# A two-layer conformer/attention trunk in fp32: other gate units of the second layer form their low parts by an adding transfer, with more raw tiles and one more weight pair

## Chip, cores and metric

One Trainium2 chip, one NeuronCore. The kernel is a single launch. The metric is the device time of that launch in microseconds (us); lower is better. Engines are named as in the profile: PE is TensorE (matmul), PEld its weight loads, DVE is VectorE, ACT is ScalarE, POOL is GpSimd, SP is SyncE, which here only issues transfers.

## What is computed

Two layers over 256 latent tokens and 256 context tokens, width 1024, all in float32. Each layer mixes tokens and then channels:

```python
h = modulate(rmsnorm(x, norm1_g[l]), sh1, sc1)
p = h @ w_in[l]                      # GLU | q, k, v | 2 x 1024 gate columns
q, k = rope_2d(q, ...), rope_2d(k, ...)
y_conv = conv_branch(p[..., :GLU_END], ...)      # GLU, depthwise conv of 31 taps, LayerNorm, swish, projection
y_attn = merge_heads(neighbourhood_attention(q, k, v, k_c, v_c, na_rpb[l])) @ w_na_out[l]
x = x + g1 * gated_merge(p[..., QKV_END:], y_conv, y_attn, w_out[l])
...
def gated_merge(p_gate, y_conv, y_attn, w_o):
    g_conv, g_attn = jnp.split(jax.nn.sigmoid(p_gate), 2, axis=-1)
    return (g_conv * y_conv + g_attn * y_attn) @ w_o
...
h2 = modulate(rmsnorm(x, norm2_g[l]), sh2, sc2)
x = x + g2 * conv_ffn(h2, w_up[l], ffn_dw[l], ffn_dw_b[l], w_down[l])
```

Context tokens go through the same weights in the first layer; in the second (the last) only their keys and values are needed. A final RMSNorm follows.

## The kernel before, in words

**Weights as units.** All weights of a layer are cut into 118 units of 128 x 1024 float32 (512 KB each), in the order in which they are used: two units of the first GLU group, four of V, thirty of the input projection (`U_IN + t`: t 0 to 5 the other GLU groups, 6 to 9 Q, 10 to 13 K, 14 to 29 the sixteen gate units), then the attention's and the conv branch's output projections (4 each), the output projection (8), up (44) and down (22).

**A product in three matmuls.** A float32 product is formed from operands split in a high part (rounded to fp32r) and a low part (the rest). `mm3` (lines 196 to 199) issues three matmuls for each 128 x 128 block: high by high (L197), high by low (L198), low by high (L199). The activations `h` are kept split; a weight unit is split when it has been loaded.

**The two ways to split a weight.** `wparts` (lines 157 to 177): SP loads the unit into a raw tile, ScalarE casts it into `whi` (L167), VectorE subtracts, `wlo = raw - whi` (L168). `wadded` (lines 211 to 219): ScalarE casts (L216), ScalarE negates the high part into `wlo` (L217), and POOL issues a transfer that adds the raw tile to `wlo` (L218); VectorE has no part in it. `unit8` picks the second way for the units in the set `ADDED` (line 47). In layer 1 these are t = 7, 8 (Q, units 1 and 2) and 16 (gate 2).

**Tiles.** The pool `w` has four raw tiles, four `whi` and four `wlo`, which all units use in turn: a new unit takes a slot when its last reader has gone. The first four up units of the second layer get their pairs from that stage's own pool `ef1` instead (argument `at`), so that all four stand at once. Each stage opens a pool of its own over the same space: `ea1` (mixing stage of layer 1: conv sums `cb`, attention outputs `oh`, `ol`, the rope table, conv inputs `u`, gates), inside it `eb1` and `ec1`, then `ef1` (feed-forward); `ef0` is the feed-forward of layer 0.

**The order of the work.** A framework orders each engine's instructions ahead of time: it takes the program's order as the priority and lets a later instruction pass an earlier one that is not ready in its own reckoning. It also sets the semaphores. On the chip each engine runs its list in order.

**Around the change.** Layer 1 begins with the two units of the first GLU group (`sc` banks), the other GLU groups, V, then Q and K of four head pairs. Between them and after them come the sixteen gate units, which fill TensorE while the attention steps wait for softmax. The 31 x 4 conv taps run on VectorE (L673) all through this stage, a few at each `slot()`. Then the attention's projection (the gates are multiplied in at L993), the layer norm of the conv branch (its first sums on POOL, L949 and L950; the sum of squares over partitions at L370), the conv projection and the merges (L998 to L1001), the output projection with residuals (L1007) and squares (L352, L356), and the feed-forward, whose first four units run on `h2` before its norm is known (L1109) and get the norm's factor later.

Of the kernel before, what the change touches and what calls it, by code (L numbers as in the profile page):

```python
# [8 lines left out]
F32 = mybir.dt.float32  # L9
F32R = mybir.dt.float32r  # L10
# [5 lines left out]
P = 128  # L16
# [15 lines left out]
UW = 1024  # L32
# [11 lines left out]

U_GLU0, U_V, U_IN, U_NA, U_CO, U_WO, U_UP, U_DN = 0, 2, 6, 36, 40, 44, 52, 96
NU = 118
ADDED = {*((0, U_IN + i) for i in (*range(19), 20, 22, 24, 26, 28)), *((0, u) for u in (U_NA + 1, U_NA + 3, *range(U_CO, U_CO + 4))), *((1, U_IN + i) for i in (7, 8, 16))}
T_GLU, T_Q, T_K, T_GATE = 0, 6, 10, 14

SWAP16 = [(i + 16) % 32 for i in range(32)]  # L50
# [3 lines left out]
def trunk(ctx: ExitStack, tc: tile.TileContext, xt, cvec, crow, wall, wada, params, bias_t, rope_t, out):  # L54
# [6 lines left out]
    wp = ctx.enter_context(tc.tile_pool(name="w", bufs=1))  # L61
# [6 lines left out]
    def nm(s):  # L68
        uid[0] += 1
        return f"{s}_{uid[0]}"  # L70
# [6 lines left out]
    def tmp(w=512):  # L77
        return tp.tile([P, w], F32, tag="t", bufs=5, name=nm("t"))
# [70 lines left out]

    lastdma = [None]  # L150

    def raw_unit(src, r=None):
        r = wp.tile([P, UW], F32, tag="raw", bufs=4, name=nm("raw")) if r is None else r
        lastdma[0] = sp.dma_start(r, src)
        return r

    def wparts(l, u, at=None, cuts=2):

        r = wp.tile([P, UW], F32, tag="raw", bufs=4, name=nm("raw"))
        hi = (at or wp).tile([P, UW], F32R, tag="whi", bufs=4, name=nm("whi"))  # L160
        lo = (at or wp).tile([P, UW], F32R, tag="wlo", bufs=4, name=nm("wlo"))
        cs = [slice(i * UW // cuts, (i + 1) * UW // cuts) for i in range(cuts)]
        for c in cs:
            lastdma[0] = sp.dma_start(r[:, c], wall[l, u][:, c])

        def split(c):
            act.copy(hi[:, c], r[:, c])  # L167
            dve.tensor_tensor(lo[:, c], r[:, c], hi[:, c].bitcast(F32), ALU.subtract)  # L168

        def more():  # L170
            for c in cs[1:]:
                split(c)

        split(cs[0])
        return (hi, lo), more

    def wunit(l, u, at=None, cuts=1):
        w, more = wparts(l, u, at, cuts)
        more()
        return w  # L180

    def cols(w, i):
        return sl(w[0], i), sl(w[1], i)
# [27 lines left out]
    def wadded(l, u):  # L211

        r = raw_unit(wall[l, u])
        hi = wp.tile([P, UW], F32R, tag="whi", bufs=4, name=nm("whi"))
        lo = wp.tile([P, UW], F32R, tag="wlo", bufs=4, name=nm("wlo"))
        act.copy(hi, r)  # L216
        act.mul(lo, hi.bitcast(F32), -1.0)  # L217
        pool.dma_start(lo, r, accum_op=ALU.add)  # L218
        return hi, lo

    def unit8(l, u, at=None):
        w = wadded(l, u) if (l, u) in ADDED else wunit(l, u, at)
        return [cols(w, i) for i in range(KD)]
# [12 lines left out]
    def ada_products(l, j, bank, place=lambda: None, after=None):  # L236

        ps = psum(bank)
        for u in range(2):
            r = raw_unit(wada[l, 2 * j + u], place())  # L240
            with tc.issue_after(after.ins) if after else ExitStack():
                ada_half(ps, u, r)
        return ps
# [45 lines left out]
    def ada_dots(l, tiles, sb, place=lambda: None, early=0):  # L289


        left, tiles, units = 0, list(tiles), []
        for i, n in enumerate(tiles):
            for m in tiles[len(units) : i + early]:
                units.append(raw_unit(wada[l, m], place()))
            while left < len(sb):
                yield
                left += pace[0]
            left -= len(sb)
            if not early:  # L300
                units.append(raw_unit(wada[l, n], place()))
            r = units[i]
            for s, v in enumerate(sb):
                dve.tensor_tensor_reduce(  # L304
                    tmp().bitcast(BF16), r, v, 1.0, pr(l, BADA + n, 1), ALU.mult, ALU.add, mods[l][:, n, s : s + 1]
                )
# [325 lines left out]
    for l in range(DEPTH):  # L632
        last = l == DEPTH - 1
# [3 lines left out]

        with ExitStack() if last else start as e1a:
            ea = e1a.enter_context(tc.tile_pool(name=f"ea{l}", bufs=1)) if last else ea0
            cb = [ea.tile([P, NS, S], F32, name=f"cb{l}_{j}") for j in range(KC)]  # L640
            oh = [ea.tile([P, T], F32R, name=f"oh{l}_{j}") for j in range(4)]
            ol = [ea.tile([P, T], F32R, name=f"ol{l}_{j}") for j in range(4)]
# [282 lines left out]
            with ExitStack() as e1c:  # L925
# [57 lines left out]
                def branch(base, xh, xl):  # L983
                    for n in range(0, KD, 2):
                        w = (wadded if (l, base + n // 2) in ADDED else wunit)(l, base + n // 2)
                        for i in range(2):
# [9 lines left out]
                for n, pc in branch(U_CO, sh_, sl_):  # L996
                    t = tmp()[:, :T]
# [56 lines left out]
                        add_side(nl)  # L1054


        with ExitStack() as e2:
            ef = e2.enter_context(tc.tile_pool(name=f"ef{l}", bufs=1))
            if not last:
# [43 lines left out]
            if last:  # L1103
# [14 lines left out]
                for i, ps in enumerate(pss):  # L1118
                    b = small([P, 1], "wb", 4)
                    act.copy(b, ps[:, S : S + 1])  # L1120
                    u = ef.tile([P, S], F32, name=f"u{l}_{i}")
# [48 lines left out]
            for streams, ns in [((0, 1), range(NB)), *(((s,), range(NB, KD)) for s in range(NS))]:  # L1170
                wu = None
                c = slice(streams[0] * S, (streams[-1] + 1) * S)
                for n in ns:
                    ps = psum()
                    for k in range(KF):
                        t = n * KF + k
# [166 lines left out]
```

## Time and profile before

| | us |
|---|---|
| median of 3 runs | 1063.33 (1061.96 to 1065.06) |
| the profiled execution | 1063.1 |
| its span, first to last instruction | 1061.3 |
| granted TensorE clock | 0.996 |

How the profile is read: "busy" is the time in which an engine had an instruction under way. Matmuls are pipelined, so a busy TensorE may still be slower than it could be; the number of matmuls in a stretch tells its rate. In rows of groups, `main<-h,whi` says which tile is written from which, with the buffer numbers left out; `xN` is the count. In rows of the timeline the first two numbers are start and duration in us, and `[0.55 <-DVE qk L882]` is the idle time ahead of the instruction and what ended it. In rows of windows the numbers in brackets are counts, and after the engines come the granted clock, the share of the transfer engines and GB/s. Rows of waits give total, number and longest.

### The profile page before, as it was taken

The numbers are of one execution on the slowest core, as the hardware profiler recorded it, in microseconds if no ns is written. First come the engines' busy times: TensorE is split into PE (matmuls) and PEld (weight loads), VectorE is DVE, ScalarE is ACT, GpSimd is POOL, SyncE is SP. The second block draws the span as 40 slices with busy tenths as digits, with TensorE's granted clock in tenths as the row PEclk, the third lists the DMA queues.
The fourth block names the chain that finished last, engine by engine and source line by source line (L and its number), as shares of the span: only waits on it lengthen the run. The fifth ranks groups of instructions, "written<-read, shape, count | busy, mean of one in ns | idle before, by whom it ended". The sixth has DMA issues, their size and how long they took to land.

```text
span 1061.3 us, 18038 instructions
## 1 busy us (share of the span) xinstructions
PE 1033.7 (97%) x6886; PEld 932.5 (88%) x6886; DVE 893.3 (84%) x1630; ACT 567.4 (53%) x943; POOL 43.6 (4%) x59
## 2 busy tenths in 40 slices
PE   8999999999999999999989999999999999999997
PEld 6787788888879988888878889999889999999997
DVE  5568898988998798898888547899899988988883
ACT  4458767545334544443433223545776666767652
POOL 1111110011000000000000000000000000000000
PEclk9999999999999999999999999999999999999998
DMA  9988665889943344564556657666734484666781
GB/s 373 304 227 229 150 153 138 260 247 245 290 149 118 101 159 160 165 190 142 186 186 218 210 189 233 208 210 196 216 117 144 159 283 155 199 205 193 230 286 61
DMA packets 59510, 209.26 MB, mean 197 GB/s; under 512 B 7200, under 2 KB 7456, under 8 KB 59424
## 3 DMA queue, kind: packets, MB, share of 16 engines
q1 hardware_dynamic: 54384, 190.77, 54.5%
q0 software_dynamic: 4752, 17.30, 8.5%
q8 instruction: 54, 0.88, 0.3%
q14 instruction: 32, 0.26, 0.1%
q10 hardware_dynamic: 288, 0.04, 0.0%
HBM read 187.63 MB, written 1.05 MB: 178 GB/s over the span
## 4 chain that ended last, share of the span: by engine, by line
PE 39%; issue 34%; DVE 16%; ACT 5%; DMA 4%; SPq 1%; POOL 0%; DVEq 0%; ACTq 0%; POOLq 0%
PE main L197 10%; PE main L198 10%; PE main L199 10%; PE main L736 4%; DVE cb L673 4%; DMA raw<-in_wall 3%; DVE wlo L168 3%; DVE t L304 2%; SPq L728 1%; ACT whi L167 1%; PE po L230 1%; DMA own<-in_wada 1%; DVE t L403 1%; DVE h L1001 1%; DVE t L999 1%
## 5 line engine op out<-in xcount | busy, mean ns | idle before, releaser
L199 PE MATMUL main<-h,wlo 128*128 128x256 f32 (+1 forms) x1328 | 430.7, 325 | 6.6 <-DVE wlo L168 6.6
L197 PE MATMUL main<-h,whi 128*128 128x256 f32 (+1 forms) x1328 | 433.5, 327 | 1.8 <-DVE qk L882 1.2
L198 PE MATMUL main<-h,whi 128*128 128x256 f32 (+1 forms) x1328 | 430.9, 325 | 1.6 <-DVE h L1001 1.4
L167 ACT CAST whi<-raw 128x1024 fp32r<-128x1024 f32 (+1 forms) x211 | 217.6, 1036 | 230.9 <-DMA raw<-in_wall 143.9
L168 DVE TENSOR_TENSOR wlo<-raw,whi 128x1024 fp32r<-128x1024 f32 (+1 forms) x211 | 252.5, 1205 | 71.7 <-ACT whi L167 70.7
L199 PEld LDWEIGHTS main<-h,wlo 128*128 128x128 f32 x1328 | 252.8, 191 | 24.9 <-DVE wlo L168 8.0
L197 PEld LDWEIGHTS main<-h,whi 128*128 128x128 f32 x1328 | 253.2, 191 | 22.9 <-issue 1.5
L198 PEld LDWEIGHTS main<-h,whi 128*128 128x128 f32 x1328 | 253.0, 191 | 19.6 <-DVE h L1001 2.1
L673 DVE SCALAR_TENSOR_TENSOR cb<-u,par,cb 128x512 f32<-128x512 f32 (+1 forms) x240 | 144.4, 617 | 2.8
L199 PE MATMUL main<-fh,wlo 128*128 128x256 f32 (+1 forms) x386 | 119.4, 309 | 0.0
L198 PE MATMUL main<-fl,whi 128*128 128x256 f32 (+1 forms) x386 | 119.3, 309 | 0.0
L197 PE MATMUL main<-fh,whi 128*128 128x256 f32 (+1 forms) x386 | 119.3, 309 | 0.0
L304 DVE CUSTOM_DVE_ANT_0 t<-raw,sb,par 128x1024 bf16<-128x1024 f32 x72 | 91.5, 1278 | 0.5 <-ACT sb L284 0.3
L199 PEld LDWEIGHTS main<-fh,wlo 128*128 128x128 f32 x386 | 73.7, 191 | 3.8 <-DVE wlo L168 0.4
L198 PEld LDWEIGHTS main<-fl,whi 128*128 128x128 f32 x386 | 73.7, 191 | 3.4
L197 PEld LDWEIGHTS main<-fh,whi 128*128 128x128 f32 x386 | 73.7, 191 | 3.4
L304 DVE CUSTOM_DVE_ANT_0 t<-own,sb,par 128x1024 bf16<-128x1024 f32 x48 | 60.4, 1279 | 2.2 <-DMA own<-in_wada 2.2
L216 ACT CAST whi<-raw 128x1024 fp32r<-128x1024 f32 x33 | 34.6, 1047 | 40.3 <-PE main L198 34.2
L1070 ACT ACTIVATE t<-main,par 128x512 f32<-128x512 f32 (+1 forms) x82 | 50.6, 666 | 5.4 <-PE main L199 5.4
L1071 DVE SCALAR_TENSOR_TENSOR t<-main,par,t 128x510 f32<-128x510 f32 (+1 forms) x82 | 47.4, 613 | 1.3 <-ACT t L1070 1.0
L1074 DVE SCALAR_TENSOR_TENSOR t<-main,par,t 128x510 f32<-128x510 f32 (+1 forms) x82 | 46.7, 611 | 0.0
L404 ACT ACTIVATE h<-t,mod 128x256 fp32r<-128x256 f32 x56 | 25.2, 501 | 33.8 <-DVE t L403 33.6
(216 smaller groups left out, 1254.7 us busy)
## 6 DMA issues: line engine op xcount, KB each, us to landing
raw<-in_wall SPq DMA_DIRECT2D x240, 512.0 KB, 4.4
raw<-in_wada SPq DMA_DIRECT2D x64, 512.0 KB, 4.4
wlo<-raw POOLq DMA_DIRECT2D x33, 512.0 KB, 5.6
own<-in_wada SPq DMA_DIRECT2D x24, 512.0 KB, 6.2
bias<-in_bias_t SPq DMA_DIRECT2D x8, 520.0 KB, 5.1
row<-in_wada SPq DMA_DIRECT2D x8, 512.0 KB, 4.8
sb<-in_crow SPq DMA_DIRECT2D x5, 512.0 KB, 4.8
x<-in_xt SPq DMA_DIRECT2D x4, 512.0 KB, 5.1
```

The costliest lines, as they stand in the source:

```text
L167: act.copy(hi[:, c], r[:, c])
L168: dve.tensor_tensor(lo[:, c], r[:, c], hi[:, c].bitcast(F32), ALU.subtract)
L197: pe.matmul(ps, w[0], order(xh), start=start, stop=False)
L198: pe.matmul(ps, w[0], order(xl), start=False, stop=False)
L199: pe.matmul(ps, w[1], order(xh), start=False, stop=stop)
L216: act.copy(hi, r)
L304: dve.tensor_tensor_reduce(tmp().bitcast(BF16), r, v, 1.0, pr(l, BADA + n, 1), ALU.mult, ALU.add, mods[l][:, n, s : s + 1])
L673: dve.scalar_tensor_tensor(cb[j], src, w, cb[j], ALU.mult, ALU.add)
L736: mm = pe.matmul(pv[t], h1[n == 1][k][:, c], runs(w[n == 2][:, b]), start=k + n == 0, stop=k == KD - 1 and n == 2)
L1070: act.activation(c, pv_, AF.Identity, bias=pr(l, FDB + t, 1), scale=w[1])
L1071: dve.scalar_tensor_tensor(c[:, :, 1:], pv_[:, :, : S - 1], w[0], c[:, :, 1:], ALU.mult, ALU.add)
L1074: dve.scalar_tensor_tensor(c[:, :, : S - 1], pv_[:, :, 1:], w[2], c[:, :, : S - 1], ALU.mult, ALU.add)
```

## The change

It does three things in layer 1.

- `ADDED` gets t = 15, 17, 19, 21, 23, 25, 27, 29 (the gate units with an odd n) and loses t = 16 (gate 2).
- A function `raw_tile` hands out raw tiles. While the mixing stage of layer 1 is being written, calls whose running number is 1, 3 or 5 modulo 7 get one of three more raw tiles in `ea1`; the others get one of the four in `w`.
- A function `split_tiles` hands out pairs. In the same stretch, every fifth call gets a pair in `ea1` (one buffer), the others one of the four in `w`.

The running numbers count all calls from the start of the program.

```diff
-ADDED = {..., *((1, U_IN + i) for i in (7, 8, 16))}
+ADDED = {..., *((1, U_IN + i) for i in (7, 8, *range(15, 30, 2)))}
...
+    more_w = [None]
+    count = [0, 0]
+
+    def raw_tile():
+        count[0] += 1
+        more = more_w[0] is not None and count[0] % 7 in (1, 3, 5)
+        return (more_w[0] if more else wp).tile([P, UW], F32, tag="raw", bufs=3 if more else 4, name=nm("raw"))
+
+    def split_tiles(at=None):
+        count[1] += 1
+        more = at is None and more_w[0] is not None and count[1] % 5 == 0
+        return [
+            (at or (more_w[0] if more else wp)).tile([P, UW], F32R, tag=t, bufs=1 if more else 4, name=nm(t)) for t in ("whi", "wlo")
+        ]
+
     def raw_unit(src, r=None):
-        r = wp.tile([P, UW], F32, tag="raw", bufs=4, name=nm("raw")) if r is None else r
+        r = raw_tile() if r is None else r
...
     def wparts(l, u, at=None, cuts=2):
-        r = wp.tile([P, UW], F32, tag="raw", bufs=4, name=nm("raw"))
-        hi = (at or wp).tile([P, UW], F32R, tag="whi", bufs=4, name=nm("whi"))
-        lo = (at or wp).tile([P, UW], F32R, tag="wlo", bufs=4, name=nm("wlo"))
+        r = raw_tile()
+        hi, lo = split_tiles(at)
...
     def wadded(l, u):
         r = raw_unit(wall[l, u])
-        hi = wp.tile([P, UW], F32R, tag="whi", bufs=4, name=nm("whi"))
-        lo = wp.tile([P, UW], F32R, tag="wlo", bufs=4, name=nm("wlo"))
+        hi, lo = split_tiles()
...
             ea = e1a.enter_context(tc.tile_pool(name=f"ea{l}", bufs=1)) if last else ea0
+            more_w[0] = ea if last else None
...
+        more_w[0] = None
         with ExitStack() as e2:
```

More of the change, by code (lines that the diff above doesn't have):

```diff
@@ L46 @@
 NU = 118
-ADDED = {*((0, U_IN + i) for i in (*range(19), 20, 22, 24, 26, 28)), *((0, u) for u in (U_NA + 1, U_NA + 3, *range(U_CO, U_CO + 4))), *((1, U_IN + i) for i in (7, 8, 16))}
+ADDED = {*((0, U_IN + i) for i in (*range(19), 20, 22, 24, 26, 28)), *((0, u) for u in (U_NA + 1, U_NA + 3, *range(U_CO, U_CO + 4))), *((1, U_IN + i) for i in (7, 8, *range(15, 30, 2)))}
 T_GLU, T_Q, T_K, T_GATE = 0, 6, 10, 14
```

## The prediction, on record before the result

> **What bounds the kernel now.** I read the page first, then the rate of TensorE, then each stage of layer 1 by windows, then what TensorE itself waited for, and last the single places.
>
> ```profile
> span 1061.3 us, 18038 instructions
> PE 1033.7 (97%) x6886; PEld 932.5 (88%) x6886; DVE 893.3 (84%) x1630; ACT 567.4 (53%) x943; POOL 43.6 (4%) x59
> q0 software_dynamic: 4752, 17.30, 8.5%
> wlo<-raw POOLq DMA_DIRECT2D x33, 512.0 KB, 5.6
> 950.00:1000.00 50.00, 50.00 (x450) 50.00 (x449) 42.78 (x74) 34.18 (x55) 0.00 (x0) 1.00 0.66 202
> 703.50:740.10 36.60, 36.60 (x219) 33.38 (x218) 36.56 (x80) 15.73 (x23) 0.92 (x1) 1.00 0.57 173
> 740.10:823.00 82.90, 81.51 (x748) 74.42 (x747) 77.76 (x186) 59.15 (x126) 4.04 (x4) 1.00 0.52 160
> 869.60:889.30 19.70, 18.23 (x152) 17.33 (x150) 16.50 (x34) 11.15 (x26) 0.70 (x1) 1.00 0.60 204
> ```
>
> The profiled execution took 1063.1 us around its span of 1061.3; the median of the runs shown, 1063.33, is 0.2 higher. In the last stretch of the feed-forward, 450 matmuls of 256 columns fill 50 us at full clock: 0.111 us each, TensorE's peak here. A gate unit of layer 1 has 24 of them, 2.67 us. From 740 to 823, where the sixteen gates and the attention lie, VectorE is busy for 77.76 of 82.90 us (94%), ScalarE for 59.15 (71%), the transfer engines for 52%. VectorE looks like the bound of this stage. But TensorE has 81.51 of the 82.90, and from 703.5 to 740.1 VectorE is full (36.56 of 36.60) without costing it anything. So the next question is what TensorE waited for.
>
> ```profile
> PE pt L370 <- DVE ss L356: 1.8, 2, 1.0
> PE main L199 <- DVE wlo L168: 1.3, 2, 0.9
> PE main L197 <- DVE qk L882: 1.2, 2, 0.6
> 769.38 0.46 PE L197 MATMUL main<-h,whi 128*128 128x512 f32 x1 [0.55 <-DVE qk L882]
> 784.88 0.38 PE L197 MATMUL main<-h,whi 128*128 128x256 f32 x1 [0.64 <-DVE qk L882]
> 829.79 0.60 PE L370 MATMUL pt<-one,ss 128*128 128x1 f32 x4 [0.97 <-DVE ss L356]
> 848.51 0.38 PE L199 MATMUL main<-h,wlo 128*128 128x256 f32 x1 [0.89 <-DVE wlo L168]
> 871.40 0.38 PE L199 MATMUL main<-h,wlo 128*128 128x258 f32 x1 [0.42 <-DVE wlo L168]
> 877.99 0.61 PE L370 MATMUL pt<-one,ss 128*128 128x1 f32 x4 [0.85 <-DVE ss L356]
> ```
>
> The first three rows are the waits of TensorE from 740 to 900, the others their places. All of it is VectorE, and all of it is 4.3 us. A late VectorE costs little because TensorE runs behind a stock of prepared weights. That is the ceiling of what the edit can win in its own stage; about 0.3% of the time, 3.2 us, is what a measurement of this kernel can tell from no change.
>
> **The change part by part: the gate units.** Eight gate units (n odd) lose their subtraction on VectorE, and gate 2, which had been without it, gets it back: seven net. The rows are the durations of a cast, the negation, the issue and the subtraction.
>
> ```profile
> L216 ACT CAST whi<-raw x33: 1027/1045/1087, 43.1 to 748.2; 128x1024 fp32r<-128x1024 f32 x33
> L217 ACT ACTIVATE wlo<-whi x33: 1042/1057/1099, 44.2 to 749.3; 128x1024 fp32r<-128x1024 f32 x33
> L218 POOL DMA_DIRECT2D wlo<-raw x33: 852/862/1058, 45.6 to 750.8; - x33
> L168 DVE TENSOR_TENSOR wlo<-raw,whi x69: 1207/1219/1231, 659.1 to 895.2; 128x1024 fp32r<-128x1024 f32 x69
> DMA to landing us min/median/max: 4.4/5.6/10.9
> ```
>
> VectorE gives up 7 x 1.22 = 8.5 us, ScalarE takes 7 x 1.06 = 7.4 us (59.15 becomes 66.6 of 82.9, 80%), POOL 7 x 0.86 = 6 us of issuing. The 33 transfers of before hold 8.5% of the span, 2.7 us of all sixteen engines each; seven more are 19 us, and the share of 0.52 becomes about 0.75. No engine becomes full.
>
> What of the 8.5 us reaches TensorE? Only the four places from 769 to 849. The one at 769.38 lies behind gate 1 (1.22 less) and gate 2 (1.22 more): no relief, 0.55 stays. The one at 784.88 follows gate 3, those at 829.79 and 848.51 follow all eight. I take 0.64 + 0.97 + 0.89 = 2.5 us as the gain. Bounds: 3.05 if 769.38 goes too; 0 if the two later ones are chains of their own (squares to root, then the burst of merges).
>
> **Is a transferred low part in time?** Cast, negation, issue and landing are 1.05 + 1.06 + 0.86 + 5.6 = 8.6 us, against 1.05 + 1.22 for a subtracted one. With four pairs a cast can start when TensorE leaves the unit four back, 3 x 2.67 = 8.0 us ahead of need; with five it is 10.7. The one example in this stage, unit 1 of Q, with four pairs:
>
> ```profile
> 732.27 1.03 ACT L216 CAST whi<-raw 128x1024 fp32r<-128x1024 f32 x1
> 734.80 0.92 POOL L218 DMA_DIRECT2D wlo<-raw  x1 [41.07 <-DVE cb L673]
> 740.52 0.38 PE L199 MATMUL main<-h,wlo 128*128 128x256 f32 x1
> SPq L164 <- DMA wlo<-raw: 9.3, 2, 5.5
> ```
>
> It was ready at about 740.5, 8.2 us after its cast began, just when TensorE came. Five pairs leave 2 us over, so I cost the longer way at nothing; the cover is those four units, and without it each transferred unit would cost 0.6 us, at the longest landing (10.9) 3.2 us. The last row is SP: raw loads queue behind a raw tile that an adding transfer still reads. With seven raw tiles instead of four, that wait has three more loads in front of it; I cost it at nothing too. On POOL the two sums of the layer norm (L949, L950) wait for the taps and stand in the same queue; whatever is issued behind them waits too.
>
> The Trainium skill (DMA: Bandwidth & Descriptors, section "Anatomy of one DMA — SWDGE (gpsimd) path") gives such a transfer 2.0 us plus its bytes at 436 GB/s, 3.2 us for 512 KB; the trace has 5.6, and by 3.2 the fifth pair would not be needed and the sum would stay as it is. A rule against the change is in SBUF — State Buffer, section "SBUF: two separate sides": VectorE in a two-port mode keeps GpSimd from writing descriptors, which would lead to rival 3. The trace shows no sign of it: VectorE at 94%, yet no issue longer than 1.06 us.
>
> **The new tiles and their pool.** The three raw tiles and the pair come from ea1, the pool of layer 1's mixing stage, whose space earlier belonged to ef0 (feed-forward of layer 0) and later to ef1. How a pool changes hands is in the trace:
>
> ```profile
> 686.71 0.28 PE L199 MATMUL main<-fhl,wlo 128*128 128x256 f32 x1
> 687.01 0.33 SPq L827 DMA_DIRECT2D rope<-in_rope_t  x1
> 849.23 0.42 DVE L999 TENSOR_TENSOR t<-t,g 128x256 f32<-128x256 f32 x1
> 849.73 0.33 SPq L282 DMA_DIRECT2D sb<-in_crow  x1
> SPq L282 <- DVE t L999: 0.8, 1, 0.8
> ```
>
> The rope table, the first load into ea1, leaves 0.02 us after the end of the last matmul that reads ef0; `sb`, the first load into ef1, leaves when the last gate of layer 1's mixing stage has been read, and waited for exactly that. I read it as a hold on the whole pool. Then two places pay.
>
> **Start of layer 1.** Pairs are counted from the first call: layer 0 makes 123 (118 units, less two that are taken by hand, plus 7 down units read twice), so layer 1 has 124 to 175, and raw tile 175 is its first. The second unit of the first GLU group is raw 176 and pair 125: both in ea1, not to be touched before 686.99.
>
> ```profile
> raw<-in_wall SPq DMA_DIRECT2D x240, 512.0 KB, 4.4
> 687.60 1.05 ACT L167 CAST whi<-raw 128x1024 fp32r<-128x1024 f32 x1 [2.31 <-DMA raw<-in_wall]
> 688.68 1.23 DVE L168 TENSOR_TENSOR wlo<-raw,whi 128x1024 fp32r<-128x1024 f32 x1
> 689.50 0.28 PE L197 MATMUL sc<-h,whi 128*128 128x256 f32 x1
> ```
>
> Its load leaves behind rope's at about 687.4, lands at 691.8, is cast by 692.9 and subtracted by 694.1; before, the pair was ready at 689.9 and TensorE came at 689.50. If TensorE's order stayed, it would stand 694.1 - 689.5 - 0.2 (two matmuls with the high part) = 4.4 us. But the next unit (raw 177, pair 126, both in the old pool) takes the freed place at 687.60, is ready at 689.9, and its 2.67 us fit in between, up to 692.6; the one after fits partly. The order of instructions is made by a scheduler that takes what is ready, as layer 0's feed-forward shows, where the code alternates between banks every six matmuls:
>
> ```profile
> 336.20:339.00 2.80, 2.69 (x22) 2.69 (x22) 0.00 (x0) 0.00 (x0) 1.00 0.00 0
> ```
>
> These are the matmuls into `sc` alone: 22 in a row. I take +1.0 us, between 0.4 and 4.4.
>
> **Start of the feed-forward.** The eighth unit of the output projection is pair 175, a multiple of five: it lies in ea1. So the first four weight pairs of the feed-forward, which go to ef1, cannot be cast before its last matmul.
>
> ```profile
> 860.20 2.15 ACT L167 CAST whi<-raw 128x1024 fp32r<-128x1024 f32 x2
> 861.82 2.35 DVE L168 TENSOR_TENSOR wlo<-raw,whi 128x1024 fp32r<-128x1024 f32 x2
> 869.48 0.28 PE L199 MATMUL main<-h,wlo 128*128 128x256 f32 x1
> 869.59 0.28 PE L197 MATMUL sc<-h,whi 128*128 128x258 f32 x1
> ```
>
> Now they are cast from 861.2 on, while the projection runs, and TensorE goes over at 869.59 with no gap. After the change the first cast starts at 869.8, its low part is done at 869.8 + 1.05 + 1.22 = 872.1, and TensorE stands 2.5 us less the two matmuls with the high part, 2.3. One unit's 24 matmuls (2.7 us) then cover the next low part (1.22). What is late next: nothing at 871.40 and 877.99, whose 0.42 + 0.85 lie inside the new wait. VectorE does 4 x 1.22 = 4.9 us more in a block with 3.2 idle (16.50 of 19.70) and 2.3 new. So +1.0. Bounds: 0 if no hold exists; if the order stays the code's, all four low parts come before the second step, 1.05 + 4 x 1.22 + 0.9 for the last square and scaling = 6.8 - 0.2 - 1.3 = +5.3.
>
> **Sum.** -2.5 + 1.0 + 1.0 = -0.5: 1062.6 us.
>
> **The rivals.** (1) *The pool's hold decides, slower.* The order stays the code's at the two starts: +4.4 + 5.3 - 2.5 = +7.2, 1070.3 us; at one of the two alone, some +3.5, 1066.6. It turns from gain to loss once the two starts together cost over 2.5. For it: both waits follow from rows above; against it, the reordering in layer 0. Chance 0.20. (2) *VectorE's lag was the whole story, faster.* The 4.3 us from 740 to 900 go, the deeper stock hides both starts: 1058.8. For it: every wait there names VectorE; against it, the 769.38 place and the two starts. Chance 0.27. (3) *Adding transfers come late, slower.* POOL's queue stands at L950 or landings go towards 10.9: 3.2 us for each such unit; two of the eight give +6.4 - 2.5 + 2.0 = +5.9, 1069.0. For it: the share of the transfer engines rises to 0.75; against it, 2 us to spare for each unit. Chance 0.08. (4) *It doesn't do what it says:* the counted rotation hands out the fifth pair at the wrong unit and the depth stays four: the 0.6 us for each of eight, +4.8, eats the gain; it falls within my forecast or rival 3, since the count is regular.
>
> **How the numbers follow.** The forecast, within 3.2 us of before, has 0.45; faster 0.27; slower 0.20 + 0.08 = 0.28. For 8 in 10 I reach down to rival 2, 1058.8, and a little below it for what the spare time of VectorE may win later, 1058.5; and up past the half of rival 1 (1066.6) to 1068.5, which leaves its full form and most of rival 3 outside.
>
> **What would show it.** Right: VectorE's busy time some 8.5 us lower, ScalarE's 7.4 higher, 40 adding transfers; 784.88 and 829.79 without their waits; the cast of the first feed-forward unit right after the projection's last matmul, and a wait of TensorE there of about 2.3 us. Wrong: no wait at either start (no hold); waits of TensorE for `wlo` of a transfer in the gate stage (rival 3); the wait at 829.79 unchanged although VectorE is freer (a chain, not a lag).

## The result and the profile after

The changed kernel is slower: 1070.23 us median of 6 runs (1066.99 to 1073.24) against 1063.18 of 6 runs of the kernel before; the ratio is 1.0068 with the interval 1.0044 to 1.0091. The forecast was 1062.6, with a range up to 1068.5. The profiled execution took 1070.85 us.

First the page's head and the row of the adding transfers' queue. The code has moved down by 13 to 15 lines: L197, L198, L199 are now L211, L212, L213, the cast L167 is L181, the subtraction L168 is L182, and the adding way is L229 to L231.

```profile
span 1069.1 us, 18057 instructions
...
PE 1039.1 (97%) x6886; PEld 937.1 (88%) x6886; DVE 886.0 (83%) x1623; ACT 574.4 (54%) x950; POOL 50.6 (5%) x66
...
q0 software_dynamic: 5760, 20.97, 10.4%
```

The work moved as counted: VectorE 893.3 to 886.0 with seven instructions fewer, ScalarE 567.4 to 574.4 and POOL 43.6 to 50.6 with seven more, and 5760 packets instead of 4752, which at 144 for a transfer are 40 instead of 33. Over the span no engine became full. Next what TensorE waited for from 680 to 900 us (total, number, longest).

```profile
PE sc L211 <- ACT whi L181: 3.9, 2, 2.7
PE pt L508 <- ACT pT L577: 1.7, 1, 1.7
PE sc L213 <- DVE wlo L182: 0.8, 1, 0.8
PE main L750 <- ACT t L705: 0.5, 1, 0.5
PE po L399 <- POOL rs L393: 0.4, 1, 0.4
PE main L211 <- ACT wb L1135: 0.3, 1, 0.3
```

The three groups that stood here before are gone: nothing for `ss`, nothing for `wlo` or `qk` in the gate stage. In their place stands ScalarE. The 3.9 us are the two starts that the prediction named; this is the timeline of the first.

```profile
687.65 0.28 PE L213 MATMUL main<-fhl,wlo 128*128 128x256 f32 x1
...
687.95 0.33 SPq L841 DMA_DIRECT2D rope<-in_rope_t  x1
688.33 10.36 SPq L178 DMA_DIRECT2D raw<-in_wall  x6
...
693.01 0.28 PE L212 MATMUL main<-h,whi 128*128 128x256 f32 x1
...
694.84 5.08 ACT L181 CAST whi<-raw 128x1024 fp32r<-128x1024 f32 x5 [5.89 <-DMA raw<-in_wall]
695.94 0.40 PE L211 MATMUL sc<-h,whi 128*128 128x256 f32 x1 [2.66 <-ACT whi L181]
```

The last matmul that reads `ef0` starts at 687.65; the rope table leaves 0.02 us after its end and the second GLU unit's raw tile behind it at 688.33. TensorE goes on with another unit (20 of its 24 matmuls, up to 693.01) and then stands. The cast it waits for starts at 694.84, when the load has landed, 6.5 us after it left. Five casts then run in one piece: ScalarE, which works its list in order, had been idle for 5.89 us ahead of the first, although the two loads that left at 684.97 and 686.90 had landed by 691.3. The same stretch by windows (busy time and count of PE, PEld, DVE, ACT, POOL, then the granted clock, the transfer engines' share, GB/s):

```profile
686.00:693.00 7.00, 7.00 (x65) 7.00 (x64) 3.03 (x5) 0.42 (x1) 1.87 (x5) 1.00 0.76 248
693.00:696.00 3.00, 0.34 (x4) 0.15 (x2) 0.08 (x1) 1.04 (x1) 0.00 (x0) 1.00 1.02 402
696.00:698.00 2.00, 2.00 (x11) 2.00 (x11) 2.00 (x2) 1.97 (x3) 0.00 (x0) 0.54 0.56 229
698.00:699.70 1.70, 1.70 (x11) 1.70 (x10) 1.70 (x3) 1.70 (x3) 0.00 (x0) 0.54 0.59 219
699.70:701.70 2.00, 2.00 (x21) 2.00 (x20) 0.91 (x1) 0.70 (x3) 0.00 (x0) 1.00 0.70 256
```

Two things are to be seen. While TensorE stands the transfer engines are full (1.02, 402 GB/s): the held loads all leave at once. And from 696 to 699.7 TensorE is "busy" all the time but begins only 18 matmuls, where 33 would fit at 0.111 us each (the counts in the rows also take in those that run over an edge): the granted clock is about a half. The wait costs 2.66 us, the half clock after it some 1.7 more, half of the 3.4 us that it lasts.

The second start, the feed-forward's, and the gate stage (timeline):

```profile
784.78 0.62 PE L508 MATMUL pt<-qk,qk 64*128 64x416 f32 x1 [1.72 <-ACT pT L577]
...
875.17 0.28 PE L213 MATMUL main<-h,wlo 128*128 128x256 f32 x1
...
875.61 1.05 ACT L181 CAST whi<-raw 128x1024 fp32r<-128x1024 f32 x1 [1.40 <-issue]
876.71 0.38 PE L211 MATMUL sc<-h,whi 128*128 128x258 f32 x1 [1.26 <-ACT whi L181]
...
877.97 0.38 PE L213 MATMUL sc<-h,wlo 128*128 128x258 f32 x1 [0.77 <-DVE wlo L182]
```

The first cast of the feed-forward starts 0.16 us after the end of the projection's last matmul, and TensorE stands 1.26 + 0.77 = 2.0 us. In the gate stage the scores (L508) wait for a bank that ScalarE has not yet read (the copy L577).

The sizes of the parts I read from the starts of the first and last matmuls of each stage in the timeline, because layer 0, the same in all these kernels, ended anywhere from 684.27 to 690.57 us in the profiles. "Start" is from the first matmul of layer 1's GLU to the last of V, "middle" from there to the last of the conv projection, "end" from there to the first down unit. In us, against the kernel before (37.25, 122.61, 146.63); "half clock" counts the episodes of half clock in layer 1 up to 900 us. These four columns are from one profiled execution of each kernel; the median is of all its runs, and the ratio is to runs of the kernel before that were measured beside them (medians 1063.18 to 1064.14).

| kernel | start | middle | end | sum | half clock | median | ratio to before |
|---|---|---|---|---|---|---|---|
| predicted | +1.0 | -1.6 | +0.1 | -0.5 | | 1062.6 | |
| the change | +5.31 | +0.09 | +1.41 | +6.81 | 2 | 1070.23 | 1.0068 (1.0044 to 1.0091) |
| both_ends | 0.00 | -1.50 | -1.47 | -2.97 | 0 | 1060.96 | 0.9976 (0.9958 to 0.9995) |
| late_start | 0.00 | -1.50 | +2.29 | +0.79 | 0 | 1064.9 | 1.0007 (0.9992 to 1.0022) |
| early_end | +3.50 | -1.51 | -1.40 | +0.59 | 0 | 1065.28 | 1.0011 (0.9991 to 1.003) |
| tiles_alone | +4.96 | +0.16 | +1.44 | +6.56 | 2 | 1069.82 | 1.0063 (1.004 to 1.0086) |
| adds_alone | 0.00 | +0.56 | +0.89 | +1.45 | 0 | 1064.92 | 1.0006 (0.9992 to 1.0021) |
| tiles_mid | 0.00 | +0.23 | -0.52 | -0.29 | 1 | 1062.61 | 0.9993 (0.998 to 1.0007) |
| start_raw | +6.10 | -1.52 | -1.10 | +3.48 | 1 | 1068.05 | 1.0042 (1.0027 to 1.0056) |
| start_pair | +0.94 | -1.50 | -1.43 | -1.99 | 0 | 1061.48 | 0.9978 (0.9969 to 0.9988) |
| end_pair | 0.00 | +0.11 | +2.39 | +2.50 | 1 | 1065.3 | 1.0013 (1.0001 to 1.0025) |
| end_raw | 0.00 | -1.52 | -2.41 | -3.93 | 0 | 1060.12 | 0.9967 (0.9953 to 0.998) |
| later_adds | 0.00 | +0.72 | -0.93 | -0.21 | 1 | 1062.0 | 0.9987 (0.9971 to 1.0003) |
| rope_late | +2.60 | +0.11 | +2.05 | +4.76 | 2 | 1068.7 | 1.0043 (1.0028 to 1.0059) |

The prediction's -2.5 is split here: 0.64 + 0.97 in the middle, 0.89 in the end.

### The profile page after: what moved, and what is told of

It is laid out like the page before. It is cut to its first block, busy times and chain, and to the rows that moved or that the text cites. A ratio compares the mean times of both kernels' runs of the same rounds, so it can differ in the third digit from the quotient of the medians.

```text
span 1069.1 us, 18057 instructions
## 1 busy us (share of the span) xinstructions
PE 1039.1 (97%) x6886; PEld 937.1 (88%) x6886; DVE 886.0 (83%) x1623; ACT 574.4 (54%) x950; POOL 50.6 (5%) x66
## 3 DMA queue, kind: packets, MB, share of 16 engines
q0 software_dynamic: 5760, 20.97, 10.4%
## 4 chain that ended last, share of the span: by engine, by line
PE 49%; DVE 23%; DMA 10%; issue 9%; ACT 7%; SPq 1%; POOLq 0%; DVEq 0%; POOL 0%; ACTq 0%
PE main L211 13%; PE main L212 13%; PE main L213 13%; DMA raw<-in_wall 8%; DVE cb L687 4%; DVE t L317 4%; DVE wlo L182 4%; PE main L750 4%; ACT whi L181 3%; DMA own<-in_wada 2%; DVE t L1086 2%; DVE t L1089 2%; SPq L742 1%; PE sc L211 1%; PE sc L212 1%
## 5 line engine op out<-in xcount | busy, mean ns | idle before, releaser
L213 PE MATMUL main<-h,wlo 128*128 128x256 f32 (+1 forms) x1328 | 431.6, 326 | 4.6 <-DVE wlo L182 4.6
L211 PE MATMUL main<-h,whi 128*128 128x256 f32 (+1 forms) x1328 | 435.1, 328 | 0.9 <-ACT h L1014 0.6
L212 PE MATMUL main<-h,whi 128*128 128x256 f32 (+1 forms) x1328 | 432.5, 326 | 1.0 <-DVE h L1015 0.7
L181 ACT CAST whi<-raw 128x1024 fp32r<-128x1024 f32 (+1 forms) x204 | 210.1, 1034 | 224.8 <-DMA raw<-in_wall 142.3
L182 DVE TENSOR_TENSOR wlo<-raw,whi 128x1024 fp32r<-128x1024 f32 (+1 forms) x204 | 243.6, 1203 | 80.1 <-ACT whi L181 79.4
L211 PEld LDWEIGHTS main<-h,whi 128*128 128x128 f32 x1328 | 254.1, 191 | 22.6 <-issue 2.2
L213 PEld LDWEIGHTS main<-h,wlo 128*128 128x128 f32 x1328 | 254.0, 192 | 22.4 <-DVE wlo L182 5.2
L212 PEld LDWEIGHTS main<-h,whi 128*128 128x128 f32 x1328 | 254.1, 192 | 19.2 <-DVE h L1015 1.8
L213 PE MATMUL main<-fh,wlo 128*128 128x256 f32 (+1 forms) x386 | 119.4, 309 | 0.8 <-DVE wlo L182 0.8
L211 PE MATMUL main<-fh,whi 128*128 128x256 f32 (+1 forms) x386 | 119.4, 309 | 0.0
L212 PE MATMUL main<-fl,whi 128*128 128x256 f32 (+1 forms) x386 | 119.3, 309 | 0.0
L213 PEld LDWEIGHTS main<-fh,wlo 128*128 128x128 f32 x386 | 73.7, 191 | 4.5 <-DVE wlo L182 1.0
L211 PEld LDWEIGHTS main<-fh,whi 128*128 128x128 f32 x386 | 73.7, 191 | 3.5
L212 PEld LDWEIGHTS main<-fl,whi 128*128 128x128 f32 x386 | 73.7, 191 | 3.4
L229 ACT CAST whi<-raw 128x1024 fp32r<-128x1024 f32 x40 | 42.0, 1049 | 40.2 <-PE main L212 32.3
L1085 ACT ACTIVATE t<-main,par 128x512 f32<-128x512 f32 (+1 forms) x82 | 50.6, 666 | 6.0 <-PE main L213 6.0
L231 POOL DMA_DIRECT2D wlo<-raw x40 | 35.0, 875 | 304.1 <-ACT wlo L230 124.0
```

The costliest lines, as they stand in the source:

```text
L211: pe.matmul(ps, w[0], order(xh), start=start, stop=False)
L212: pe.matmul(ps, w[0], order(xl), start=False, stop=False)
L213: pe.matmul(ps, w[1], order(xh), start=False, stop=stop)
L1085: act.activation(c, pv_, AF.Identity, bias=pr(l, FDB + t, 1), scale=w[1])
```

## The experiments

Two theories were set against each other: the *hold* (the new tiles lie in a pool whose space is not free at both ends of the stage) and the *late adding transfers*, the prediction's third rival.

**Undoing one end or both.** `both_ends` uses the new tiles only from the V projection to the conv projection; `late_start` undoes the start alone, `early_end` the end alone.

```diff
-            more_w[0] = ea if last else None
...
                     glu_groups(2)
                     rate[0] = 3
+                    more_w[0] = ea
...
+                more_w[0] = None
                 sss = sum_squares(NS, S)
```

The first two edits are `late_start`, the last is `early_end`, all three are `both_ends`.

> The change, but the three raw tiles and the pair of ea1 are handed out only from V of layer 1 (after the GLU groups) to the conv branch's projection, not for the first GLU groups and not for the output projection. Theory H (the hold on the whole pool makes both starts wait): the 4.5 us of the stretch from the first GLU unit to V and about 1 us at the feed-forward go, some 5.5 us below the changed kernel, about 1064.5. Rival D (the adding transfers crowd the raw loads wherever they are): nothing changes, about 1070.

> Only the start undone: ea1's tiles are handed out from V on, but still for the output projection. H: 4.5 us below the changed kernel, about 1065.5, and the first GLU unit to V takes 16.8 us again instead of 21.3; the first cast of the feed-forward still starts behind the projection's last matmul. D: no change, 1070.

> Only the end undone: ea1's tiles are handed out from the first GLU unit on, but no longer for the output projection. H: about 1 us below the changed kernel, 1069, with the start still 21.3 us long and no wait of TensorE for the first cast of the feed-forward. Were the feed-forward's start the larger part of the loss, it would be 5 us below.

All three bear the hold out, though not its expected sizes: `both_ends` was expected at 1064.5 and `early_end` at 1069, so the end's part was taken too small. Each end undone alone brings the time from 1070.2 to 1065, both bring it to 1061, below the kernel before, with all eight transferred gates in place. By the medians, the start's hold costs 4.3 us and the end's 3.9. All that TensorE waits for in `both_ends` from 680 to 900:

```profile
PE pt L508 <- ACT pT L577: 1.7, 1, 1.7
PE po L399 <- POOL rs L393: 0.3, 1, 0.3
```

**The tiles without the transfers, the transfers without the tiles.** `tiles_alone` keeps the old set, `adds_alone` never sets the flag.

```diff
-... *((1, U_IN + i) for i in (7, 8, *range(15, 30, 2)))}
+... *((1, U_IN + i) for i in (7, 8, 16))}
```

> The new tiles with the old choice of units (gate 2 alone adds by transfer). H: both holds stay, so 5 to 6 us slower than before, 1069, and VectorE's waits in the gate stage stay as before or shrink by the deeper stock. S (ScalarE's 7.4 us more is what costs): about as before, 1063. D: about as before, 1063.

> The eight transferred gates with the four raw tiles and four pairs of before; nothing lies in ea1 or is held. Pool's hold: start of layer 1 (16.8 us from the first GLU matmul to the first V matmul) and of the feed-forward as before; in the gate stage VectorE's waits (3.1 us) go, but a transferred low part takes 8.2 to 8.6 us with four units (8.0) of cover, so 0 to 0.6 us each is paid: 1061 to 1066, ratio to before 0.998 to 1.003. Adding transfers late (rival 3): waits of TensorE for a transferred wlo in the gate stage, 1066 or more. If instead the gain of both_ends came from the deeper stock and not from the transfers, this one is not below before.

```diff
-            more_w[0] = ea if last else None
+            more_w[0] = None
```

`tiles_alone` is as slow as the change (1069.82 against 1070.23): the loss needs none of the eight transfers, and the late-transfers theory falls. `adds_alone` is level with before. Its waits of TensorE, 686 to 900:

```profile
PE pt L383 <- DVE ss L369: 2.1, 2, 1.6
PE main L213 <- DVE wlo L182: 1.2, 2, 0.9
PE sc L508 <- ACT pT L577: 1.1, 2, 0.6
...
PE main L213 <- DMA wlo<-raw: 0.3, 1, 0.3
```

Only 0.3 us of it is a transferred low part, so four pairs nearly suffice. But of the three places whose waits the prediction counted as its gain, only the one for `qk` is gone. The other two, which were 0.97 and 0.89 us before, are here:

```profile
829.76 0.61 PE L383 MATMUL pt<-one,ss 128*128 128x1 f32 x4 [0.57 <-DVE ss L369]
848.49 0.38 PE L213 MATMUL main<-h,wlo 128*128 128x256 f32 x1 [0.89 <-DVE wlo L182]
```

Freeing VectorE did not by itself remove them, and waits for ScalarE (`pT`, `pp`) of 1.9 us in all came up in the attention.

**The tiles in the middle alone.** `tiles_mid` is `both_ends` with the old set.

> Like both_ends (more tiles from the V projection to the end of the closing convolution only), but with the three transferred units of before. If both_ends gains by the tiles' depth: its 1061, ratio 0.998. If it gains by the transfers, which need the tiles: the VectorE waits of before (1.8 + 0.6 + 0.9 us) come back and the time is that of before, 1063 to 1064, ratio 1.000. The hold theory asks that both starts cost nothing here: 16.8 us to the first V matmul, no wait of the feed-forward's first cast for the projection.

Its median is not clear of before (0.9993), and its interval overlaps that of `both_ends` (0.9976), so the times alone do not tell whether the tiles gain without the transfers. Its waits say more:

```profile
PE sc L508 <- ACT pT L577: 2.2, 1, 2.2
PE main L213 <- DVE wlo L182: 0.8, 1, 0.8
PE po L399 <- POOL rs L393: 0.6, 1, 0.6
```

All three waits that the prediction counted are gone, for `qk`, for `ss` and for the first `wlo` of the output projection, although VectorE subtracts as much as before; the `wlo` left (at 871.91) belongs to the first units of the feed-forward. The copy has come. The middle stands at +0.23 with one episode of half clock in it; without that (some 1.7 us, an estimate) it would be about -1.5, as in `both_ends`. So in the middle the gain comes with the tiles; the end is where `both_ends` is better, -1.47 against -0.52.

**Raw tile or pair, at the start.** `start_raw` is `both_ends` with raw tiles in `ea1` from the first GLU group on (raw 176, the second GLU unit's, then 178 and 180 of later groups), `start_pair` with the second GLU unit's pair there. The pairs get a flag of their own, `more_p`. Against `both_ends`, shown for `start_raw`, one of the two flags is set at the old place again; `start_pair` sets `more_p` there instead of `more_w`.

```diff
-        more = at is None and more_w[0] is not None and count[1] % 5 == 0
+        more = at is None and more_p[0] is not None and count[1] % 5 == 0
...
+            more_w[0] = ea if last else None
...
-                    more_w[0] = ea
+                    more_w[0] = more_p[0] = ea
```

> both_ends, but the raw tile of the second GLU unit lies in ea1 again (its weight pair does not). If the late load is what costs at the start (held until the last matmul of ef0, landing with six others): the stall of TensorE for the cast stays, 20 to 21 us to the first V matmul, some 1065, ratio to both_ends 1.003 to 1.004. If the pair's hold costs: 16.8 us and 1061.

> both_ends, but the weight pair of the second GLU unit lies in ea1 again (its raw tile does not). If the late load is what costs: the raw tile lands as before, the cast can start at the last matmul of ef0 and the low part is there 2.3 us later, about when TensorE comes, so 16.8 to 17.5 us to the first V matmul and 1061 to 1062. If the pair's hold costs: 20 to 21 us and some 1065.

The load is what costs: 1068.05 against 1061.48. In `start_raw` the start is 6.1 us longer, more than expected; the timeline and a window show of what:

```profile
689.74 0.58 PE L384 MATMUL pt<-one,ss 128*128 128x1 f32 x4 [0.87 <-DVE ss L370]
691.43 0.43 PE L400 MATMUL po<-ident,rs 128*128 128x128 f32 x2 [1.11 <-POOL rs L394]
692.75 3.89 ACT L182 CAST whi<-raw 128x1024 fp32r<-128x1024 f32 x4 [4.44 <-DMA raw<-in_wall]
693.85 0.58 PE L212 MATMUL sc<-h,whi 128*128 128x256 f32 x1 [1.99 <-ACT whi L182]
...
693.90:696.00 2.10, 2.10 (x9) 2.08 (x10) 2.10 (x2) 2.10 (x3) 0.00 (x0) 0.50 0.63 256
```

The cast waits for the landing, 6.5 us after the last `ef0` matmul ended (686.20 to 692.75); TensorE's list has no other unit here to fill the gap, so two chains of the norm show beside it, and the half clock follows. In `start_pair` the pool is free from 687.60, the cast that TensorE waits for starts at 689.62, behind another cast and a square in ScalarE's list, and the wait is 0.4 us. The first load behind the rope table, here one of another unit, landed 4.9 us after it left, with the next load leaving only 2.6 us behind it; in the change it was 6.4 us, with three more loads leaving within 1.5 us.

**The queue at the start.** `rope_late` is the change with the rope table's load behind that of the held raw tile.

```diff
-                    sp.dma_start(rope, rope_t)
                     pg0 = [psum("sc") for _ in range(2)]
...
+                    sp.dma_start(rope, rope_t)
                     glu(0, *pg0)
```

> The change itself, with one edit: the load of the rope table leaves behind that of the held raw tile and not ahead of it, so the raw tile is the first of the held loads. If half of the late landing (6.4 us against the usual 4.4) is the place in the queue and the table's 256 KB: it lands 0.5 to 1 us sooner, and 0.5 to 1.5 us of the 21.3 us to the first V matmul go (with less of the halved clock): 1069 to 1070. If the five loads on the way from before it make it late: nothing changes, 21 us and 1070.

The cast starts 6.06 us after the start of the last `ef0` matmul instead of 7.19: 1.1 us sooner for one place in the queue and 256 KB. The wait is only 0.5 us shorter, yet the start came out 2.7 us shorter, because in this profile no half clock and no lag in V followed it. (The intervals of the two ratios overlap, so the times alone do not show a gain.)

```profile
696.25 0.38 PE L211 MATMUL sc<-h,whi 128*128 128x256 f32 x1 [2.19 <-ACT whi L181]
...
696.00:698.00 2.00, 1.75 (x14) 1.69 (x15) 1.23 (x1) 1.20 (x3) 0.00 (x0) 1.00 1.01 414
```

**Raw tile or pair, at the end.** `end_pair` is `both_ends` with the projection's pairs 170 and 175 (its third and eighth unit) in `ea1`, `end_raw` with raw tiles of the projection there.

```diff
-                more_w[0] = None
+                more_p[0] = None
                 sss = sum_squares(NS, S)
```

That is `end_raw`; `end_pair` clears `more_w[0]` there instead.

> both_ends, but the weight pair of the output projection's eighth unit (and no raw tile of the projection) lies in ea1 again. If that pair is what holds ef1, as the prediction said: the first cast of the feed-forward starts only after the projection's last matmul, TensorE waits about 2.3 us there, and the stretch from the closing convolution's last matmul to the end of the first four feed-forward units is 2 to 3 us longer than in both_ends (34.5 us): some 1063 to 1064. If raw tiles hold it, 34.5 us and 1061.

> both_ends, but raw tiles of the output projection's units lie in ea1 again (no pair of them does). A raw tile has been read when its low part is made, some units ahead of the projection's last matmul, so if the pair holds ef1 this costs at most some tenths: 34.5 to 35 us in that stretch, 1061. If raw tiles hold it: 36.5 us or more, 1063 to 1064.

The pair holds it: 37.7 us from the conv projection's last matmul to the end of the first four up units against 34.5 in `both_ends`, and these waits from 840 to 900 us:

```profile
PE sc L212 <- ACT whi L182: 1.3, 1, 1.3
PE po L400 <- POOL rs L394: 0.8, 1, 0.8
PE sc L214 <- DVE wlo L183: 0.8, 1, 0.8
PE main L212 <- ACT wb L1137: 0.5, 1, 0.5
```

In `end_raw` TensorE has no wait at all in that stretch, the 34.5 become 33.5, and the median is the lowest measured here: 1060.12, ratio 0.9967. Raw tiles in that pool are read early and hold nothing. By the profile more of them in the projection are even a gain of 0.9 us, which was not expected; the intervals of the two kernels overlap.

**The wait that came instead.** Every kernel with the new tiles in the gate stage waits 1.7 to 2.2 us for a copy of ScalarE in the attention. `later_adds` is `both_ends` with gates 1 and 3 subtracted again and gate 2 transferred, so that ScalarE has less to do ahead of it.

```diff
-... *((1, U_IN + i) for i in (7, 8, *range(15, 30, 2)))}
+... *((1, U_IN + i) for i in (7, 8, 16, *range(19, 30, 2)))}
```

> both_ends, but gates 1 and 3 subtract again and gate 2 adds, as before, so ScalarE has 1.06 us less to do ahead of the attention's copies near 783 us. If ScalarE's load by the transferred units makes the wait of 1.7 us of TensorE for the copy there, it shrinks by about 1 us and the V projection to cross-attention stretch goes from 98.2 to about 97.2: 1060. If that wait belongs to the order of the instructions and not to the load, it stays, and the time is that of both_ends, 1061, or up to 1 us more where VectorE's wait at 785 comes back.

```profile
PE pt L508 <- ACT pT L577: 1.7, 1, 1.7
PE po L399 <- POOL rs L393: 0.7, 1, 0.7
PE sc L508 <- ACT pT L577: 0.6, 1, 0.6
```

The wait stays 1.7 us, and a second of 0.6 comes beside it. So it is not ScalarE's load by these two units. The long wait comes with the tiles: `tiles_mid` has it without the transfers, and `adds_alone`, without the tiles, has three waits for the copy of at most 0.6 us. Why the tiles bring it is open.

## Why the prediction was wrong

- *Gates.* Nearly right in size once the ends are out of the way, but not in the cause. Without them (`both_ends`) the middle and the end gain 1.50 + 1.47 = 3.0 us; forecast were 2.5, from 0 to 3.05, because VectorE has seven subtractions fewer. The three waits of VectorE went, as listed under what would show it. But they also went in `tiles_mid`, with none of the subtractions saved, and in `adds_alone`, with all of them saved, only the one for `qk` did: it is the deeper stock of tiles that removes them. The transfers show at the feed-forward's start, where the prediction set them at nothing: `tiles_mid` waits there for 0.77 (`wlo`) and 0.62 us (`rs`), `both_ends` for 0.33 (`rs`). So the fit of 2.5 and 3.0 is in part luck. A wait of 1.7 us for ScalarE's copy came, which the prediction did not see; in the profile of the change the half clock after it took away the rest, and the middle ended at +0.09. The third rival fell.
- *Start of layer 1: the step that failed.* The prediction took +1.0 between 0.4 and 4.4; the profile has +5.31. The hold, the units (raw 176, pair 125) and the other unit that fills the gap were right: 20 of its 24 matmuls ran ahead. Three sizes were wrong. The load was taken to land 4.4 us after leaving, the median of all loads; it took 6.4, since the other held-up loads left with it and filled the transfer engines. The casts of the units behind it were taken as free to go ahead; ScalarE works in order and did five in a row after it, and "the one after", which was to fit partly (raw 178, 3 modulo 7), was held itself. And nothing was set for the clock, which fell to a half for 3.4 us after the wait. The wait, 2.66, plus some 1.7 of half clock, plus 0.76 in V (0.5 of it TensorE's wait for `t`) make 5.1 of the 5.3.
- *Start of the feed-forward.* The mechanism was exact (pair 175, the first cast right after the last matmul, a wait of 2.3 us forecast and 2.0 seen), the size too small. For projection and feed-forward together +0.1 was forecast and +1.41 measured. Beside the wait, what `both_ends` gains there was lost: 2.9 us lie between the two, and 3.9 between `end_pair` and `both_ends`, of which 0.4 to 0.7 come only later, in the other up units.
- *The first rival* gave 1070.3, and the kernel came out at 1070.23, but not by its terms. It had both orders staying as the code has them, with +4.4, +5.3 and -2.5. At the start the order did change; the parts measured are +5.3, +0.1 and +1.4. That the figure fits is chance; its statement, that the holds outweigh the gain, is what the runs confirmed; it had been given 0.20.

The differences add up: (5.31 - 1.0) + (0.09 + 1.6) + (1.41 - 0.1) = 7.3 us between the forecast's -0.5 and the measured +6.8. The rest of the difference of the spans, 0.9 us, lies in layer 0, whose code did not change.

One reading of the trace of before was also wrong, without harm to the sum: the cast at 687.60, with a low part done at 689.9, is not the second GLU unit's but that of a later one. TensorE begins on the second unit at 689.50, and its third matmul there, which needs the low part, ran ahead of 689.9:

```profile
689.72 0.28 PE L199 MATMUL sc<-h,wlo 128*128 128x256 f32 x1
```

Counted back from the last cast, the second unit's was the one at 681.54, and its pair was ready at 687.0.

## What to carry to other kernels

Extra buffers taken from another stage's space are not free at that stage's ends: look which load is the first into them and which reader the last out, and switch them off there; here three lines turned a loss of 0.7% into a gain of 0.2%. Price a held load by the crowd that leaves with it, and a held cast by all that stands behind it on its engine. A wait of TensorE of 2 us should be priced at up to 3.7, for the half clock that may follow. And a forecast gain that arrives is no proof of its cause: here the runs with the tiles alone and with the transfers alone showed that the waits went with the tiles, not with the work taken off VectorE.

## What the runs showed of the hardware

The clock after a wait was not expected. In the gate stage the same wait of 1.72 to 1.73 us stands in the change and in `both_ends`, and only one is followed by the half clock. First the change, then `both_ends`, each the 2 us after the wait:

```profile
784.80:786.80 2.00, 2.00 (x9) 1.50 (x10) 0.79 (x4) 2.00 (x5) 0.33 (x1) 0.53 0.77 279
```

```profile
782.40:784.40 2.00, 1.99 (x17) 1.74 (x18) 0.79 (x4) 2.00 (x5) 0.31 (x1) 1.00 0.83 279
```

In the layer-1 part up to 900 us of the kernel before, the change and the twelve experiments there were ten episodes, each 3.41 us long by the clock's record in the trace and at half clock, so worth some 1.7 us; nine came with a single wait of 1.7 to 2.7 us of TensorE. Of the seventeen such waits nine were followed by one and eight were not, at like lengths. The tenth stands at the feed-forward's start in `rope_late`, where the wait is split in two. This is also how I read that the stretch from the last matmul of V to the attention's projection, of the same code, is 98.2 us long in `both_ends` and `end_raw` and 99.8 in `end_pair`.

The record also shows what sets the eight apart. In each profile the episodes begin on a grid of 3.413 us: in the change at 549.39, 696.17 and 784.91, which are 43 and 26 steps apart. What counts is the idle time of TensorE within one step. First the change, where the whole wait (783.06 to 784.78) lies in one step, then `both_ends`, where the end of a step cuts it (780.68 to 782.41):

```profile
781.50:784.91 3.41, 1.69 (x26) 1.23 (x24) 3.34 (x11) 1.65 (x5) 0.00 (x0) 1.00 1.01 154
784.91:788.32 3.41, 3.41 (x16) 2.91 (x17) 2.20 (x9) 3.04 (x8) 0.86 (x1) 0.50 0.82 278
```

```profile
778.21:781.62 3.41, 2.47 (x32) 1.72 (x30) 3.34 (x9) 1.65 (x4) 0.68 (x1) 1.00 0.78 131
781.62:785.04 3.42, 2.63 (x23) 2.38 (x24) 2.21 (x7) 3.20 (x8) 0.86 (x1) 1.00 0.80 214
```

An episode earlier in each of the fourteen profiles places its grid. In layer 1 up to 900 us every step with 1.72 us idle or more was followed by an episode (ten of ten), and none with 1.71 or less was; that is about half a step. In layer 0 the border is less sharp: a step with 1.36 us idle was followed by one, a step with 1.86 was not, and why is open. Where the grid lies against the program differs from one profile to the next, so whether a given wait of this length is followed by an episode is luck.

The Trainium skill (TensorE: Matmul & The Clock Gate, section "Part 1: The HAM clock gate (the "warmup" mystery)") describes a free-running window of about 3.4 us by which the clock is either full or half. Length, depth and grid of the episodes agree with it. But its table names a whole idle window as the condition for the half clock; here some 1.72 us idle, half of one, were enough.
